# Attention keys and queries stored as half-precision pairs instead of fp32r pairs, with a power of two on the keys and its inverse on the queries

## The chip, the cores and the metric

The kernel runs on one core of one Trainium2 chip. The metric is device time in microseconds of one execution. The kernel before was timed three times: 3205.57 us is the median, 3202.81 and 3209.93 us are the ends. One further execution was taken by the hardware profiler; all rows in this document come from such profiled executions.

TensorE (PE in the rows) multiplies; a weight load (PEld) puts the stationary operand into the array before each product. VectorE is DVE, ScalarE is ACT, GpSimd is POOL, and SP is the queue from which most DMAs are issued; POOL issues the others.

## The reference, cut to what matters

Two layers over 2048 tokens of width 1024: a Mamba-2 mixer, then a multi-head latent attention of 16 heads. The part that the change touches is the score of the second layer:

```
ckv, k_rope = split(rms_norm(h, g_kv_in) @ w_dkv, [256])
kv = (rms_norm(ckv, g_ckv) @ w_ukv).reshape(B, S, 16, 64 + 64)
k_nope, v = split(kv, [64]);  k_rope = apply_rope(k_rope, cos, sin)
q = (rms_norm(cq, g_q) @ w_uq).reshape(B, S, 16, 64 + 32)
q_nope, q_rope = split(q, [64]);  q_rope = apply_rope(q_rope, ...)
s = einsum(q_nope, k_nope) + einsum(q_rope, k_rope)      # 96 channels in all
p = softmax(where(mask, s * 96 ** -0.5, -inf));  o = einsum(p, v)
```

So every head has keys and queries of 96 channels (64 of its own, 32 turned by the rotary table, of which the keys' 32 are shared by the heads), and a causal mask. Inputs and output are float32.

## The kernel before, in words

**Pairs.** A product in high precision is made of three passes on TensorE: each operand is a pair of a rounded value (hi) and what the rounding left (lo), and `mm3` (lines 84 to 88) adds hi·hi, hi·lo and lo·hi into one bank of PSUM. Its lines 86, 87 and 88 are therefore the lines of nearly all large products. Two kinds of pairs are in use. `split` (lines 106 to 113) makes pairs in F32R, four bytes each: ScalarE writes hi, VectorE subtracts (lines 109 and 110, or 112 and 113 with a scale). `pair16` (lines 115 to 118) makes pairs in F16, two bytes each, always with a scale (lines 117 and 118). Mamba's projections, the values V and the probabilities are F16 pairs already; keys and queries are F32R pairs.

**Mamba, about the first 1570 us.** The tokens are cut into 4 blocks of 512 (b), the channels into 4 groups (g); the 16 items (b, g) follow each other in the loop of lines 339 to 369. Beside the state-space scan `ssd` of its item, which has 4 chunks of 5 steps, an iteration emits the output product of the item before (`outp`, 8 steps) and the projections of the item after (`xbc` and `zgate`, together 24 steps). Generators listed in `parts` are run one after the other; after each of their steps, as many steps of `ssd` are emitted as keep `done * total` up with `20 * step`, so the 20 scan steps are spread evenly over `total` steps of the parts. At b = 0, g = 0 and 1, `scan` adds 11 steps that hold no product but one: they load weights, square them on ScalarE with a running sum (line 180) and turn the sum into a power of two (`powers`). In the last block `value_scale` does the like for the values. The order of instructions on each engine comes from a planner, which follows this order of emission as a priority and its own view of durations; the kernel writes no order by hand here. Raw weights pass through the buffer `wraw`, which has 3 slots.

**Latent attention's projections, about 1570 to 2089 us.** For each block of 512 tokens, `mla_kv_down`, `mla_cq`, `mla_up` and `mla_gate` make the latents, the keys, queries and values, and the gate. In `mla_up`, `out` (lines 883 to 886) takes a product of 128 channels by 512 tokens from PSUM, splits it and stores the pair into DRAM through the POOL queue: `kn_d` for the keys, `qn_d` for the queries. `rope` (lines 770 to 781) does so for the turned channels: `kr_d`, `q1_d` and `q2_d`.

**Attention, about 2089 to 3010 us.** For each of 16 heads, `load_k` and `load_q` (lines 939 to 958, POOL queue) bring the head's keys (96 partitions, 2 halves, 2048 tokens) and queries (96, 2, 512 per block) into SBUF, a head ahead of their use. `heads` walks over 4 blocks of 512 queries, each in 4 rows of 128. `cuts` cuts the keys that a row sees into tiles of 512, with a shorter end of 256, 384 or 512; the narrowest width is 256 columns, `max(w, 256)`. That makes 40 tiles in a head: 25 of 512 columns, 7 of 384 and 8 of 256, of which one, the head's first, needs only 128 but is computed with 256. Of every tile:

- `mm3` computes the scores with the queries as weights and the keys as the moving operand (lines 86 to 88, rows `mm<-K,xT`); the last tile of a row gets the mask added by one more product (line 1016, and line 1014 for the head's first tile);
- VectorE takes the maximum (line 1017), then the row's maximum (line 1021);
- ScalarE takes the exponential with its sum (line 1029);
- TensorE transposes it in 128x128 pieces (line 1044), ScalarE and VectorE make an F16 pair of it (lines 117 and 118, rows `PTs<-tr`), and two products with V add into the head's output (lines 1054 and 1055).

TensorE's order in this stage is written by hand: `CREDIT` says after which score tile how many transposes (T) and value products (V) are issued. The orders of VectorE and ScalarE come from the planner. Score tiles and transposes share 8 banks of PSUM, so TensorE can run ahead of ScalarE by few tiles only.

**The output projection** takes the rest, from about 3010 us, and is not touched.

Of the kernel before, what the change touches and what calls it, by code (L numbers as in the profile page):

```python
# [69 lines left out]
class Net:  # L70
# [180 lines left out]
    def constants(self, cp):  # L251
        nc, a = self.nc, self.a
        self.pack = cp.tile([P, PACK], F32, name="pack")
        self.idb = cp.tile([P, P], BF16, name="idb")

        self.mk = cp.tile([P, 2 * P], BF16, name="mk")
        at = 0
        for name, n in PACKED:
            setattr(self, name, self.pack[:, at:at + n])
            at += n  # L260

    def layer_constants(self, cp):
# [12 lines left out]
        nc.vector.memset(self.halfpi, TWO_PI / 4)  # L275
        nc.vector.memset(self.mk[:, P:], NEG)
# [3 lines left out]
        self.xdown = cp.tile([P, 1], F32, name="xdown")  # L280
        self.dtdown = cp.tile([P, 1], F32, name="dtdown")
        ss = self.t(self.sm, "ss", [P, 3, 4], bufs=2)[:, 0, :2]
# [13 lines left out]
        nc.vector.tensor_copy(self.idb, self.ident)  # L296
        nc.vector.tensor_copy(self.mk[:, 0:P], self.mask)

# [14 lines left out]
    def mamba(self, cp):  # L313
# [25 lines left out]
        for n, (b, g) in enumerate(items):  # L339
# [32 lines left out]
    def value_scale(self):  # L372
# [4 lines left out]
        for n in range(2):  # L377
# [24 lines left out]
            yield  # L402

    def load_x(self, b, src, tag="hx"):
# [364 lines left out]

    def rope(self, p1, p2, cos, sin, d1, d2, n, t0):  # L770
# [45 lines left out]
    def mla_kv_down(self, b, tables):  # L816
# [10 lines left out]
        for j in range(2):  # L827
# [3 lines left out]
            pk.append(ps)  # L831
        self.rope(pk[0], pk[1], *tables, self.kr_d[0:16], self.kr_d[16:32], 16, b * TB)

# [36 lines left out]
    def mla_up(self, b, tables):  # L870
# [28 lines left out]
        while ahead:  # L899
            (n, w), ahead = ahead, next(todo, None)  # L900
            qT = self.qT
            for i in range(2 if n == 6 else 4):
                r0 = n % 2 * 512 + i * P
                if n < 2:
                    out(chan(cT, w, i, "tr"), self.kn_d[r0:r0 + P])
                elif n < 4:
# [67 lines left out]
    def heads(self, sp):  # L974
# [4 lines left out]
        def cuts(kv):  # L979

            out, at = [], 0
            while at < kv:
                w = min(TB, kv - at)
                if kv - at == TB + P:
                    w = 384
                out.append((at, max(w, 256)))
                at += w
            return out

        def scores(h, qb, st):  # L990
# [8 lines left out]
            for j in range(4):  # L999
# [5 lines left out]
                for n, (c0, w) in enumerate(parts):  # L1005
# [6 lines left out]
                    if n == nb - 1:  # L1012
                        if qb == j == 0:
                            nc.tensor.matmul(s[:, 0:w], self.idb, self.mk, start=False, stop=True)
                        else:
                            nc.tensor.matmul(s[:, w - P:w], self.idb, self.mk[:, 0:P], start=False, stop=True)
                    v.tensor_reduce(mx[:, n:n + 1], s[:, :w], AX.X, ALU.max)  # L1017
# [208 lines left out]
    def run(self):  # L1226
        tc = self.tc
        with ExitStack() as whole:
# [8 lines left out]
            self.ri_d = dp.tile([NH, T], F32, name="ri_d")  # L1237
            self.qn_d = dp.tile([1024, 2, T], F32, name="qn_d")
            self.q1_d = dp.tile([256, 2, T], F32, name="q1_d")
            self.q2_d = dp.tile([256, 2, T], F32, name="q2_d")  # L1240
            self.kn_d = dp.tile([1024, 2, T], F32, name="kn_d")
            self.kr_d = dp.tile([32, 2, T], F32, name="kr_d")
            self.v_d = dp.tile([T, 2048], F16, name="v_d")
# [59 lines left out]
```

## Time and profile before

| | us |
|---|---|
| median of 3 runs | 3205.57 |
| the profiled execution's own time | 3204.34 |
| span of that execution, first to last instruction | 3202.6 |
| Mamba | 0 to 1570 |
| latent projections | 1570 to 2089 |
| attention | 2089 to 3010 |
| output projection | 3010 to 3202.6 |

The mean granted TensorE clock was 0.995 of full speed. A row of a group names the line, the engine, the operation, the output and the inputs with their shapes, the count, the busy time in us with the mean of one in ns, and the idle time of the engine just before, with what ended it. A row of a window gives its length and each engine's busy time in it with the number of instructions, then the granted clock, the share of the DMA engines and their rate. A matmul's shown duration includes a latency that overlaps the next one's, so two durations are compared by their difference, or starts are compared with starts.

### The profile page before, as it was taken

The numbers are of one execution on the slowest core, as the hardware profiler recorded it, in microseconds if no ns is written. First come the engines' busy times: TensorE is split into PE (matmuls) and PEld (weight loads), VectorE is DVE, ScalarE is ACT, GpSimd is POOL, SyncE is SP. The second block draws the span as 40 slices with busy tenths as digits, with TensorE's granted clock in tenths as the row PEclk, the third lists the DMA queues.
The fourth block names the chain that finished last, engine by engine and source line by source line (L and its number), as shares of the span: only waits on it lengthen the run. The fifth ranks groups of instructions, "written<-read, shape, count | busy, mean of one in ns | idle before, by whom it ended". The sixth has DMA issues, their size and how long they took to land.

```text
span 3202.6 us, 51345 instructions
## 1 busy us (share of the span) xinstructions
PE 3085.4 (96%) x17744; PEld 2163.4 (68%) x17744; DVE 2401.2 (75%) x5178; ACT 1914.1 (60%) x4817; POOL 609.1 (19%) x842
## 2 busy tenths in 40 slices
PE   6999999999999999999999999999999999999998
PEld 3455555666655566665878888877777777777777
DVE  7778887767677676767876665678888888888675
ACT  8667554444455444455645554477877778778522
POOL 0212122121122212212111211322212122222100
PEclk9999999999999999999999999999999999999999
DMA  8667645334443345334476656853444434443485
GB/s 285 229 214 230 229 144 194 127 126 145 141 157 130 115 151 189 127 128 142 141 271 218 225 190 194 265 111 78 95 81 84 81 78 96 79 97 99 101 270 159
DMA packets 207113, 497.61 MB, mean 155 GB/s; under 512 B 27746, under 2 KB 51042, under 8 KB 205412
## 3 DMA queue, kind: packets, MB, share of 16 engines
q1 hardware_dynamic: 165444, 370.04, 35.6%
q0 software_dynamic: 41408, 124.29, 15.9%
q8 instruction: 140, 2.29, 0.3%
q14 instruction: 121, 0.99, 0.1%
HBM read 362.22 MB, written 131.99 MB: 154 GB/s over the span
## 4 chain that ended last, share of the span: by engine, by line
PE 64%; DVE 13%; ACT 8%; DMA 8%; issue 6%; POOL 1%; SPq 0%; ACTq 0%; DVEq 0%; POOLq 0%
PE mm L86 13%; PE mm L87 12%; PE mm L88 12%; PE tr L1044 6%; PE tr L87 3%; PE tr L1054 3%; PE tr L1055 3%; PE tr L86 3%; PE tr L88 3%; DVE cacc L460 3%; DMA big<-cumT 2%; DMA wraw<-in_ssm_w_in_dram 1%; DVE big L634 1%; ACT Pr L1029 1%; PE tr L656 1%
## 5 line engine op out<-in xcount | busy, mean ns | idle before, releaser
L118 DVE SCALAR_TENSOR_TENSOR PTs<-tr,PTs 128x512 f16<-128x512 f32 (+3 forms) x640 | 374.9, 607 | 93.9 <-ACT PTs L117 86.8
L117 ACT ACTIVATE PTs<-tr 128x512 f16<-128x512 f32 (+3 forms) x640 | 328.5, 541 | 141.4 <-PE tr L1044 140.3
L1017 DVE TENSOR_REDUCE mx<-mm 128x1 f32<-128x512 f32 (+2 forms) x631 | 375.7, 608 | 45.7 <-PE mm L88 42.6
L1029 ACT ACTIVATE Pr<-mm,nm 128x512 f32<-128x512 f32 (+2 forms) x631 | 395.7, 636 | 23.1 <-DVE nm L1021 21.4
L1044 PE MATMUL tr<-pack,Pr 128*128 128x128 f32 x2176 | 317.6, 273 | 1.0 <-ACT Os L1061 0.9
L86 PE MATMUL mm<-K,xT 96*128 96x512 f32 (+2 forms) x639 | 288.2, 451 | 23.3 <-ACT Pr L1029 21.8
L86 PE MATMUL mm<-xT,wsp 128*128 128x512 f16 (+1 forms) x800 | 304.9, 381 | 0.3 <-DVE sz L484 0.3
L88 PE MATMUL mm<-xT,wsp 128*128 128x512 f16 (+1 forms) x800 | 303.4, 380 | 1.4 <-DVE wsp L118 1.3
L87 PE MATMUL mm<-xT,wsp 128*128 128x512 f16 (+1 forms) x800 | 303.7, 380 | 0.0
L1044 PEld LDWEIGHTS tr<-pack,Pr 128*128 128x128 f32 x2176 | 253.5, 141 | 49.7 <-ACT Os L1061 1.7
L648 ACT ACTIVATE Xw<-tr,d_wend 128x64 f32<-128x64 f32 x512 | 183.4, 359 | 133.3 <-DVE Xd L644 133.3
L460 DVE SCALAR_TENSOR_TENSOR cacc<-craw,pack,cacc 128x512 f32<-128x512 f32 x288 | 213.6, 764 | 30.5 <-ACT cacc L458 28.9
L86 PE MATMUL mm<-wsp,xT 128*128 128x512 f16 (+1 forms) x640 | 232.4, 363 | 1.6 <-ACT craw L454 1.6
L88 PE MATMUL mm<-K,xT 96*128 96x512 f32 (+2 forms) x639 | 231.6, 362 | 0.0
L87 PE MATMUL mm<-wsp,xT 128*128 128x512 f16 (+1 forms) x640 | 231.6, 362 | 0.0
L87 PE MATMUL mm<-K,xT 96*128 96x512 f32 (+2 forms) x639 | 231.4, 362 | 0.0
L88 PE MATMUL mm<-wsp,xT 128*128 128x512 f16 (+1 forms) x640 | 231.1, 362 | 0.0
L1054 PE MATMUL tr<-PTs,xT 128*128 128x512 f16 (+3 forms) x640 | 222.0, 348 | 0.1
L86 PE MATMUL mm<-wsp,yT 128*128 128x512 f32 x512 | 208.1, 409 | 13.3 <-DVE sz L484 4.7
L1055 PE MATMUL tr<-PTs,xT 128*128 128x512 f16 (+3 forms) x640 | 219.4, 347 | 0.0
L606 POOL TENSOR_TENSOR Xp<-Xw,Xp 128x512 fp32r<-128x512 f32 x64 | 81.8, 1278 | 711.3 <-ACT Xp L605 382.4
L88 PE MATMUL mm<-wsp,yT 128*128 128x512 f32 x512 | 203.0, 397 | 1.4 <-DVE yT L110 1.4
(411 smaller groups left out, 7418.2 us busy)
## 6 DMA issues: line engine op xcount, KB each, us to landing
wsp<-wi_d SPq DMA_DIRECT2D x96, 512.0 KB, 3.7
wsp<-wo_d SPq DMA_DIRECT2D x96, 512.0 KB, 3.5
big<-cumT SPq DMA_DIRECT2D x64, 512.0 KB, 4.9
wi_d<-wsp SPq DMA_DIRECT2D x32, 512.0 KB, 3.4
wo_d<-wsp SPq DMA_DIRECT2D x64, 256.0 KB, 2.5
xT<-qn_d POOLq DMA_DIRECT2D x64, 256.0 KB, 4.4
K<-kn_d POOLq DMA_DIRECT2D x15, 1024.0 KB, 9.2
hx<-in_ssm_w_in_dram SPq DMA_DIRECT2D x48, 256.0 KB, 4.3
```

The source lines that it names most:

```text
L86: mm(out, l_hi, r_hi, start=start, stop=False)
L87: mm(out, l_hi, r_lo, start=False, stop=False)
L88: mm(out, l_lo, r_hi, start=False, stop=stop)
L117: self.nc.scalar.activation(hi, src, AF.Copy, scale=scale)
L118: self.nc.vector.scalar_tensor_tensor(lo, src, scale, hi, ALU.mult, ALU.subtract)
L460: nc.vector.scalar_tensor_tensor(acc, raw[:, k:k + TB], wk[k], acc, ALU.mult, ALU.add)
L648: act(Xw[:, hc], px[:, hc], AF.Copy, scale=wend[:, h0 + h:h0 + h + 1])
L1017: v.tensor_reduce(mx[:, n:n + 1], s[:, :w], AX.X, ALU.max)
L1029: nc.scalar.activation(x[:, :w], s[:, :w], AF.Exp, bias=nm, accum_out=sm[:, n:n + 1])
L1044: nc.tensor.transpose(pt[:, j * P:(j + 1) * P], st["P"][j][kb], self.ident)
L1054: nc.tensor.matmul(st["O"][:, c], vals[h][:, kb, :], u[:, 0], start=kb == 0, stop=False)
L1055: nc.tensor.matmul(st["O"][:, c], vals[h][:, kb, :], u[:, 1], start=False, stop=kb == nk - 1)
```

## The change

Keys and queries become F16 pairs. The DRAM arrays `kn_d`, `kr_d`, `qn_d`, `q1_d`, `q2_d` and the SBUF tiles `K` and `xT` of the queries are F16; `out` and `rope` call `pair16` in place of `split`. So that neither side leaves the range of F16, the keys are multiplied by one power of two, `ku`, in `pair16`'s scale, and the queries by its inverse, which is multiplied into `gqs`, the gain that the query latents have anyway. `ku` is computed by a new generator `head_scale` from the weights' squared sums, as one more part of the item b = 1, g = 0. It has 22 steps and counts 22 in `total`: 21 loads (13 of 128x512, 8 of 128x32) through `wraw` with a square on ScalarE each, and one step of small operations with one tiny product. In `cuts` the least width of 256 is gone, so that the head's first tile has 128 columns, the wide mask tile is gone with its line 1014, and `mk` is half as wide.

```diff
@@ mamba
+            if b == 1 and g == 0:
+                parts.append(self.head_scale())
+                total += 22
@@
+    def head_scale(self):
+        nc, v, a = self.nc, self.nc.vector, self.a
+        ss = self.t(self.sm, "hs", [P, 3, 12], bufs=1)
+        pieces = [(0, a["kv_w_up"][k * P:(k + 1) * P, c * TB:(c + 1) * TB], self.gkl[:, k:k + 1])
+                  for k in range(2) for c in range(2)]
+        pieces += [(2, a["mla_w_uq"][k * P:(k + 1) * P, c * TB:(c + 1) * TB], self.gqs[:, k:k + 1])
+                   for k in range(3) for c in range(3)]
+        pieces += [(1, a["kv_w_down"][k * P:(k + 1) * P, 256:288], self.gk[:, k:k + 1]) for k in range(KD)]
+        at = [0, 0, 0]
+        for i, src, gain in pieces:
+            n = src.shape[1]
+            raw = self.t(self.wp, "wraw", [P, TB], bufs=WRAW)
+            nc.sync.dma_start(raw[:, :n], src)
+            nc.scalar.activation(self.t(self.sp, "yt", [P, D], BF16, bufs=2)[:, :n], raw[:, :n], AF.Square,
+                                 scale=gain, accum_out=ss[:, i, at[i]:at[i] + 1])
+            at[i] += 1
+            yield
+        x = self.t(self.sm, "hx", [P, 2], bufs=1)
+        for i in range(3):
+            v.tensor_reduce(ss[:, i, 0:1], ss[:, i, :at[i]], AX.X, ALU.add)
...
+        nc.tensor.matmul(ps[:, 0:2], self.ones, x, start=True, stop=True)
...
+        v.tensor_scalar(self.ku.bitcast(I32), e[:, 2:3], 23, None, ALU.logical_shift_left)
...
+        v.tensor_scalar(self.gqs, self.gqs, x[:, 0:1], None, ALU.mult)
+        yield
@@ rope (and the call for the keys passes self.ku[:16])
-            u = self.ev()
-            self.split(u[:n, 0, :], u[:n, 1, :], x[:n])
-            nc.gpsimd.dma_start(d[:, :, t0:t0 + TB], u[:n].bitcast(F32))
+            u = self.ev(F16)
+            self.pair16(u[:n, 0, :], u[:n, 1, :], x[:n], scale)
+            nc.gpsimd.dma_start(d[:, :, t0:t0 + TB], u[:n])
@@ mla_up (and the call for the keys passes self.ku)
-        def out(ps, d):
-            u = self.ev()
-            self.split(u[:, 0, :], u[:, 1, :], ps)
-            nc.gpsimd.dma_start(d[:, :, t0:t0 + TB], u.bitcast(F32))
+        def out(ps, d, scale=1.0):
+            u = self.ev(F16)
+            self.pair16(u[:, 0, :], u[:, 1, :], ps, scale)
+            nc.gpsimd.dma_start(d[:, :, t0:t0 + TB], u)
@@ load_k, load_q
-            self.keys[h] = self.t(self.hp, "K", [96, 2, T], F32R, bufs=2)
+            self.keys[h] = self.t(self.hp, "K", [96, 2, T], F16, bufs=2)
-        Q = self.quer[h, n] = self.t(self.xq, "xT", [96, 2, TB], F32R, bufs=8)
+        Q = self.quer[h, n] = self.t(self.xq, "xT", [96, 2, TB], F16, bufs=8)
@@ cuts
-                out.append((at, max(w, 256)))
+                out.append((at, w))
@@ scores
-                        if qb == j == 0:
-                            nc.tensor.matmul(s[:, 0:w], self.idb, self.mk, start=False, stop=True)
-                        else:
-                            nc.tensor.matmul(s[:, w - P:w], self.idb, self.mk[:, 0:P], start=False, stop=True)
+                        nc.tensor.matmul(s[:, w - P:w], self.idb, self.mk, start=False, stop=True)
@@ run: qn_d, q1_d, q2_d, kn_d, kr_d
-            self.kn_d = dp.tile([1024, 2, T], F32, name="kn_d")
+            self.kn_d = dp.tile([1024, 2, T], F16, name="kn_d")
```

More of the change, by code (lines that the diff above doesn't have):

```diff
@@ L254, in constants @@
         self.idb = cp.tile([P, P], BF16, name="idb")
-        self.mk = cp.tile([P, 2 * P], BF16, name="mk")
+        self.mk = cp.tile([P, P], BF16, name="mk")
         at = 0
@@ L275, in layer_constants @@
         nc.vector.memset(self.halfpi, TWO_PI / 4)
-        nc.vector.memset(self.mk[:, P:], NEG)
         self.wdt = cp.tile([P, KD, 2, H], F16, name="wdt")
@@ L280, in layer_constants @@
         self.xdown = cp.tile([P, 1], F32, name="xdown")
+        self.ku = cp.tile([P, 1], F32, name="ku")
         self.dtdown = cp.tile([P, 1], F32, name="dtdown")
@@ L296, in layer_constants @@
         nc.vector.tensor_copy(self.idb, self.ident)
-        nc.vector.tensor_copy(self.mk[:, 0:P], self.mask)
+        nc.vector.tensor_copy(self.mk, self.mask)
     def layers(self):
@@ L768, in rope_tables, with rope @@
         return cos, ang
-    def rope(self, p1, p2, cos, sin, d1, d2, n, t0):
+    def rope(self, p1, p2, cos, sin, d1, d2, n, t0, scale=1.0):
         nc, v = self.nc, self.nc.vector
@@ L831, in mla_kv_down @@
             pk.append(ps)
-        self.rope(pk[0], pk[1], *tables, self.kr_d[0:16], self.kr_d[16:32], 16, b * TB)
+        self.rope(pk[0], pk[1], *tables, self.kr_d[0:16], self.kr_d[16:32], 16, b * TB, self.ku[:16])
     def mla_cq(self, b):
@@ L904, in mla_up @@
                 if n < 2:
-                    out(chan(cT, w, i, "tr"), self.kn_d[r0:r0 + P])
+                    out(chan(cT, w, i, "tr"), self.kn_d[r0:r0 + P], self.ku)
                 elif n < 4:
@@ L1237, in run @@
             self.ri_d = dp.tile([NH, T], F32, name="ri_d")
-            self.qn_d = dp.tile([1024, 2, T], F32, name="qn_d")
-            self.q1_d = dp.tile([256, 2, T], F32, name="q1_d")
-            self.q2_d = dp.tile([256, 2, T], F32, name="q2_d")
-            self.kn_d = dp.tile([1024, 2, T], F32, name="kn_d")
-            self.kr_d = dp.tile([32, 2, T], F32, name="kr_d")
+            self.qn_d = dp.tile([1024, 2, T], F16, name="qn_d")
+            self.q1_d = dp.tile([256, 2, T], F16, name="q1_d")
+            self.q2_d = dp.tile([256, 2, T], F16, name="q2_d")
+            self.kn_d = dp.tile([1024, 2, T], F16, name="kn_d")
+            self.kr_d = dp.tile([32, 2, T], F16, name="kr_d")
             self.v_d = dp.tile([T, 2048], F16, name="v_d")
```

11 lines of the change are left out of this document (added).

## The prediction, made before the changed kernel was run

> **What bounds the kernel now.** I read the page's busy shares first, then the windows by stage and by head, then the groups of attention with shapes kept apart, and last the timeline of a few microseconds.
>
> ```profile
> PE 3085.4 (96%) x17744; PEld 2163.4 (68%) x17744; DVE 2401.2 (75%) x5178; ACT 1914.1 (60%) x4817; POOL 609.1 (19%) x842
> ...
> core 0: us, PE busy (x) PEld busy (x) DVE busy (x) ACT busy (x) POOL busy (x), PEclk, DMA share, GB/s
> 1570.00:2089.00 519.00, 508.74 (x2542) 432.09 (x2541) 337.51 (x668) 266.60 (x503) 97.58 (x158) 1.00 0.68 223
> 2555.00:2612.30 57.30, 56.03 (x356) 42.99 (x354) 48.30 (x115) 45.38 (x128) 12.07 (x19) 1.00 0.42 84
> ```
>
> TensorE is the bound: busy for 96% of the span, the next engine for 75%. In attention one head takes 57.2 us, of which it is busy 56.0; VectorE is next with 48.3. A saving on TensorE there is worth its full size until VectorE's 48.3 us, or the order in which the engines wait for each other, comes in the way.
>
> Is a busy TensorE at its own limit, or held by its weight loads? The timeline of two short stretches answers:
>
> ```profile
> 2500.29 0.38 PE L1055 MATMUL tr<-PTs,xT 128*128 128x512 f16 x1
> ...
> 2500.32 0.59 PE L86 MATMUL mm<-K,xT 96*128 96x512 f32 x1
> ...
> 2500.74 0.40 PE L87 MATMUL mm<-K,xT 96*128 96x512 f32 x1
> ...
> 2510.74 0.28 PE L86 MATMUL mm<-K,xT 96*128 96x256 f32 x1
> 2510.86 0.28 PE L87 MATMUL mm<-K,xT 96*128 96x256 f32 x1
> ```
>
> Passes of 256 columns start 120 ns apart. And L86 shows 0.59 us only because its start is shown early: from the start of L1055 to the start of L87 lie 0.45 us, which hold both passes.
>
> **Term 1, the score passes.** The same product with F16 operands is in the trace, in the value products next door:
>
> ```profile
> L1055 PE MATMUL tr<-PTs,xT 128*128 128x512 f16 x448 | 169.8, 379 | 0.0
> L87 PE MATMUL mm<-K,xT 96*128 96x512 f32 x395 | 155.6, 394 | 0.0
> L1016 PE MATMUL mm<-mk,idb 128*128 128x128 bf16 x238 | 54.9, 231 | 0.0
> L87 PE MATMUL mm<-K,xT 96*128 96x384 f32 x110 | 37.1, 337 | 0.0
> L86 PE MATMUL mm<-K,xT 96*128 96x256 f32 x126 | 38.1, 302 | 0.6 <-ACT Pr L1029 0.5
> L87 PE MATMUL mm<-K,xT 96*128 96x256 f32 x126 | 35.6, 283 | 0.0
> L1055 PE MATMUL tr<-PTs,xT 128*128 128x384 f16 x64 | 20.9, 326 | 0.0
> L1055 PE MATMUL tr<-PTs,xT 128*128 128x256 f16 x64 | 17.4, 273 | 0.0
> L1055 PE MATMUL tr<-PTs,xT 128*128 128x128 f16 x64 | 14.0, 219 | 0.0
> L1014 PE MATMUL mm<-mk,idb 128*128 128x256 bf16 x15 | 4.2, 283 | 0.0
> ```
>
> The durations hold the same overlapped latency, so their differences are the saving of a pass. 512 columns: 394 - 379 = 15 ns; 400 tiles of 3 passes give 18.0 us. 384: 337 - 326 = 11 ns; 112 x 3 gives 3.7 us. 256: 283 - 273 = 10 ns; 112 x 3 gives 3.4 us. The head's first tile goes from 256 to 128 columns: 302 + 2 x 283 + 283 ns (with its mask product) become three times 219 and 231, 263 ns less, 4.2 us over 16 heads. The sum is 29 us. If the 450 ns above less 2 x 215 is right for L86, each triple has some 5 ns more, so I put the upper end at 33 us.
>
> How much of it arrives? TensorE has a gap of 1.3 us in each head (57.3 less 56.03). What ends it stands in the first row below: an exponential on ScalarE frees the bank of the next score tile. That exponential waits for the row's maximum, and that for the row's last product; no F16 pass lies in this chain behind that product, so I leave the gap as it is. In the densest stretch, the second row, VectorE has little to give:
>
> ```profile
> L86 PE MATMUL mm<-K,xT 96*128 96x512 f32 x395 | 202.2, 512 | 22.5 <-ACT Pr L1029 21.3
> ...
> 2536.00:2546.00 10.00, 10.00 (x72) 8.14 (x69) 9.35 (x29) 8.59 (x27) 0.85 (x2) 1.00 0.64 129
> ```
>
> A head would lose 29/16 = 1.8 us, 3%; in this stretch 0.3 us of 10, and VectorE has 0.65. It fits, but barely, since both engines wait for each other in turn. I take 25 of 29 us; the lower end is 12, where more than half of each head gives nothing. VectorE's and ScalarE's orders are replanned and could differ by some tenths of a microsecond per head either way; that is inside these ends.
>
> The weight loads of the score passes get shorter too, though by the starts above they lie under the passes and count nothing in this term:
>
> ```profile
> L87 PEld LDWEIGHTS mm<-K,xT 96*128 96x128 f32 x631 | 120.1, 190 | 8.4
> L1055 PEld LDWEIGHTS <-xT 128*128 128x128 f16 x640 | 62.7, 98 | 14.8 <-issue 0.2
> ```
>
> The Trainium skill, in TensorE: Matmul & The Clock Gate, under Weight-path perf modes, says that a full load of 128 weights that aren't FP32 goes by a fast path, measured as about twice as fast. The trace agrees with the speed, 98 against 190 ns; what it would make of the time, were the loads in the way, is one of the rivals below.
>
> **Term 2, the new part head_scale.** It gives TensorE nothing to do but one tiny product, and it stretches the scan of item (1, 0): with 54 steps in place of 32, only 20 x 32 / 54, 12 of the 20 scan steps, are emitted beside the projections; 8 come beside loads and squares alone. What lies behind is `outp` of the same item, which needs the scan's results. The like exists in items (0, 0) and (0, 1): there 35 steps with 24 of products leave 6 uncovered, and 43 with 32 leave 5.
>
> ```profile
> 157.00:187.00 30.00, 22.96 (x146) 17.29 (x144) 23.34 (x70) 25.87 (x71) 3.85 (x4) 0.87 0.88 275
> 260.00:292.00 32.00, 25.92 (x163) 19.10 (x162) 25.70 (x74) 28.03 (x73) 2.60 (x2) 0.95 0.85 282
> 536.00:566.00 30.00, 29.38 (x168) 15.63 (x166) 24.30 (x53) 17.44 (x41) 8.31 (x11) 1.00 0.30 99
> ...
> 167.00:172.00 5.00, 5.00 (x33) 4.12 (x30) 2.07 (x5) 3.16 (x9) 1.28 (x1) 0.50 0.73 232
> ```
>
> The ends of (0, 0) and (0, 1) idle 7.0 and 6.1 us against 0.6 at the end of (1, 0) today, and in the first the clock fell to 0.50 for 5 us, which cost another 2.5. So 9.5 us over 6 steps and 6.1 over 5, 1.6 and 1.2 us for each. With 8 steps that would be 10 to 13 us. But those ends also had 85% of the DMA engines in use, longer squares and weight splits in ScalarE's queue (28 us busy of 32, against 17 of 30 in the third row), so I take 9 us. The lower end is 2 us: ScalarE has 12 idle us in the third row's stretch and may square early. The upper end is where the loads go round one after another: 21 loads through 3 slots are 7 rounds, each a landing and a square.
>
> ```profile
> hx<-in_ssm_w_in_dram SPq DMA_DIRECT2D x48, 256.0 KB, 4.3
> ...
> L180 ACT ACTIVATE yt<-hx 128x1024 bf16<-128x1024 f32 x30 | 31.8, 1064 | 3.9 <-DMA hx<-in_ssm_w_in_dram 2.1 <-DVE y L663 1.8
> L239 ACT ACTIVATE yt<-xs 128x384 bf16<-128x384 f32 x16 | 8.2, 527 | 0.1
> ```
>
> About 4.3 us and, for 512 columns, some 0.7 us with the sum's reading: 5 us a round, 35 us. Less 3 us of products of `outp` that are ready by then (I put them at 12 passes of 0.23 us), that is 32. On SP's queue the 21 loads stand ahead of later weight loads and of the scan's `big<-cumT`; on ScalarE the scan's operations stand behind a square that waits for its load. That is how the upper end would come about.
>
> The Trainium skill says under The HAM clock gate of the same page that TensorE's clock goes to half after an idle window of about 3.4 us. The window at 167 agrees: granted clock 0.50 after the gaps ahead of it; by that rule alone, one long gap at the end of item (1, 0) would cost a few microseconds beyond itself.
>
> **Term 3, eviction, stores and loads.** `pair16` in place of `split`:
>
> ```profile
> L109 ACT ACTIVATE big<-mm 128x512 fp32r<-128x512 f32 x12 | 7.2, 599 | 9.4 <-PE mm L88 9.2
> L117 ACT ACTIVATE big<-tr 128x512 f16<-128x512 f32 x12 | 7.1, 596 | 5.7 <-PE tr L88 4.8 <-ACT xs L863 0.7
> L112 ACT ACTIVATE yT<-tr,pack 128x512 fp32r<-128x512 f32 x12 | 7.4, 692 | 0.0
> ```
>
> 596 for 599 ns, and VectorE subtracts from PSUM as before: nothing for the queries. With a scale from a tile ScalarE takes about 692, so 32 stores of keys cost 3 us there, beside TensorE, which is the bound of that stage with 508.7 of 519 us while ScalarE has 266.6. Were that cover gone, it would be those 3 us. Stores and loads move half the bytes on the POOL queue; attention's idle TensorE waits for no DMA in any row of term 1, and the stage before idles 10 us in all. I take 0, from 3 us won to 3 lost.
>
> **The sum.** Against the profiled execution's own 3204.34 us: -25 + 9 + 0 = 3188.3. The runs' median lies 1.2 us above that execution, so 3189.5, rounded to 3189.
>
> **The rivals.**
>
> Replanned order (chance 0.16): VectorE's queue is in order, and an exponential or a maximum planned behind a pair that waits for transposes holds the next score tile; then each head's gap grows by what the passes save. For it: the dense stretch, VectorE 9.35 of 10. Against: 48.3 of 57.3 over a head. With 10 of 29 us arriving: 3205.57 - 10 + 9, about 3204, no change.
>
> The loads of head_scale go one after another (0.09): the upper end of term 2, at the end of item (1, 0), about 540 to 600 us. It decides once that idle time passes 25 us. For it: three slots, squares queued between the scan's operations. Against: for the loads of `scan`, ScalarE waited 2.1 us over 30 squares. Then 3205.57 - 25 + 32 + 2.5 for the halved clock, about 3215, slower.
>
> Weight loads in the way (0.07): if the 118 ns by which L86's mean duration exceeds L87's (512 against 394) were load and not an early shown start, part would go with faster loads: 92 ns (190 - 98) on 640 tiles, 59 us more, so about 3131. Against it: the 450 ns for two passes above. This is what the rule of Weight-path perf modes in the Trainium skill's page would come to here.
>
> head_scale is absorbed (0.10): term 2 near 2 us and term 1 near 29; about 3178.
>
> **How the numbers follow.** The forecast itself has 0.58, and its own range from the ends of the terms is 3175 to 3200. About 0.2% (6.4 us) is what a measurement of this kernel can tell from no change. Faster than 3199.2: 0.56 of the forecast's 0.58, the absorbed case, the weight loads, together 0.73. Within: 0.02 of the forecast and 0.14 of the replanned order, 0.16. Slower: the loads and 0.02 of the replanned order, 0.11. The range of 8 in 10 is 3170 to 3207: it takes in the replanned order and leaves out the weight loads and the serial loads.
>
> **What would show it.** Term 1: rows `mm<-K,xT` in F16 with 380 ns for lines 87 and 88, weight loads of 98 ns, a head of about 55.6 us in place of 57.2, and a gap per head still near 1.3 us; a gap of 3 us would be the replanned order. Term 2: the window of 30 us that ends with item (1, 0) idles about 9 us and its clock dips. Term 3: the stage of the projections stays at 519 us. The forecast is wrong if the head shrinks by under 0.8 us, or if item (1, 0) and the next lose over 20 us.

## The result, and the profile after

The changed kernel takes 3185.82 us, the median of four runs (3185.80 to 3190.25); the kernel before took 3204.94 us beside it (3202.81 to 3209.93). The ratio is 0.9942, with a 95% interval of 0.9924 to 0.9959. So the kernel became 19 us faster; the prediction said 3189.

The page of the kernel after has this row of busy shares:

```profile
PE 3059.6 (96%) x17746; PEld 2046.3 (64%) x17746; DVE 2394.7 (75%) x5191; ACT 1929.9 (61%) x4859; POOL 610.5 (19%) x842
```

TensorE is the bound as before, with 26 us less of busy time, and the busy time of its weight loads fell by 117 us. The time is in four places, which the windows cut at the same events show: the start of item (1, 0), where `head_scale` is, to the start of item (1, 1); from there to the start of item (1, 3); from Mamba's last product to the first score; from the first score to the start of the last head's closing transpose (line 1073 before, 1110 after). Columns are as in the prediction's windows (length, busy time of PE, PEld, DVE, ACT and POOL with their instructions, clock, DMA share, GB/s). First the kernel before:

```profile
475.80:566.50 90.70, 89.75 (x535) 54.08 (x534) 64.03 (x127) 44.70 (x120) 19.94 (x24) 1.00 0.55 188
566.50:771.50 205.00, 201.70 (x1173) 124.63 (x1172) 144.97 (x295) 95.55 (x253) 37.85 (x48) 0.99 0.38 129
1553.80:2088.00 534.20, 523.46 (x2647) 444.40 (x2645) 350.24 (x697) 280.37 (x539) 101.28 (x163) 1.00 0.68 222
2088.00:3011.80 923.80, 899.40 (x5654) 686.89 (x5654) 772.71 (x1831) 733.59 (x2009) 201.82 (x296) 1.00 0.42 84
```

Then the kernel after; the fifth row is one head:

```profile
475.20:587.40 112.20, 101.06 (x568) 62.01 (x567) 64.24 (x130) 56.78 (x162) 16.82 (x24) 0.94 0.55 184
587.40:784.40 197.00, 192.84 (x1140) 117.50 (x1140) 145.92 (x308) 95.39 (x253) 38.24 (x48) 1.00 0.39 134
1567.40:2093.10 525.70, 522.88 (x2646) 445.87 (x2645) 352.62 (x697) 283.64 (x539) 106.63 (x170) 1.00 0.57 183
2093.10:2993.80 900.70, 871.55 (x5656) 567.37 (x5654) 763.79 (x1831) 734.27 (x2009) 198.97 (x289) 1.00 0.27 60
...
2556.00:2611.60 55.60, 54.14 (x354) 35.33 (x353) 47.45 (x115) 45.29 (x126) 12.16 (x19) 1.00 0.29 58
```

| stretch | before | after | difference | forecast |
|---|---|---|---|---|
| item (1, 0) and the next two | 295.7 | 309.2 | +13.5 | +9 |
| latent projections | 534.2 | 525.7 | -8.5 | 0 |
| attention | 923.8 | 900.7 | -23.1 | -25 |
| all the rest | | | -0.4 | 0 |
| profiled execution's own time | 3204.34 | 3185.83 | -18.5 | -16 |

Item (1, 0) alone lost 21.5 us, but 33 of TensorE's instructions moved into it from the items behind (535 to 568 in the first row, 1173 to 1140 in the second), so these two rows are read together. Attention gave what was forecast, `head_scale` took half as much again, and the projections gave something that wasn't forecast. The products themselves look as foretold, with shapes kept apart:

```profile
L86 PE MATMUL mm<-K,xT 96*128 96x512 f16 x395 | 150.1, 380 | 24.3 <-ACT Pr L1066 22.4
...
L87 PE MATMUL mm<-K,xT 96*128 96x512 f16 x395 | 149.4, 378 | 0.0
L1053 PE MATMUL mm<-mk,idb 128*128 128x128 bf16 x253 | 55.9, 221 | 0.0
```

And the loads of their weights, in the page's costliest groups:

```profile
L87 PEld LDWEIGHTS <-xT 96*128 96x128 f16 (+1 forms) x1152 | 112.7, 98 | 153.7 <-issue 65.0
```

378 ns for line 87 where 394 stood; 380 for line 86 where 512 stood; 98 ns for a load where 190 stood. The mask's product (line 1053, was 1016) is shorter too, 221 for 231 ns, though nothing in it was changed. The idle time in front of a score tile is still ended by the exponential, 24.3 us where it was 22.5. By these rows alone one would say: the forecast's mechanism, and nothing else. The experiments show that this is not so.

### The profile page after: what moved, and what is told of

Its sections match the earlier page's. It is cut to its first block, busy times and chain, and to the rows that moved or that the text cites. A ratio compares the mean times of both kernels' runs of the same rounds, so it can differ in the third digit from the quotient of the medians.

```text
span 3184.1 us, 51344 instructions
## 1 busy us (share of the span) xinstructions
PE 3059.6 (96%) x17746; PEld 2046.3 (64%) x17746; DVE 2394.7 (75%) x5191; ACT 1929.9 (61%) x4859; POOL 610.5 (19%) x842
## 4 chain that ended last, share of the span: by engine, by line
PE 64%; DVE 13%; ACT 8%; DMA 6%; issue 6%; POOL 1%; SPq 1%; ACTq 0%; DVEq 0%; POOLq 0%
PE mm L86 13%; PE mm L87 12%; PE mm L88 12%; PE tr L1081 6%; PE tr L87 4%; PE tr L86 4%; PE tr L88 3%; PE tr L1092 3%; PE tr L1091 3%; DVE cacc L500 3%; ACT Pr L1066 2%; DMA big<-cumT 2%; DMA wraw<-in_ssm_w_in_dram 1%; DVE PTs L118 1%; DVE big L674 1%
## 5 line engine op out<-in xcount | busy, mean ns | idle before, releaser
L86 PE MATMUL mm<-K,xT 96*128 96x512 f16 (+2 forms) x639 | 222.8, 349 | 27.2 <-ACT Pr L1066 23.7
L88 PE MATMUL mm<-K,xT 96*128 96x512 f16 (+2 forms) x639 | 222.5, 348 | 0.0
L87 PE MATMUL mm<-K,xT 96*128 96x512 f16 (+2 forms) x639 | 221.7, 347 | 0.0
L86 PE MATMUL mm<-wsp,yT 128*128 128x512 f32 x512 | 208.4, 410 | 11.9 <-DVE sz L524 6.3
L87 PEld LDWEIGHTS <-xT 96*128 96x128 f16 (+1 forms) x1152 | 112.7, 98 | 153.7 <-issue 65.0
```

Of the source, the lines that this page charges most:

```text
L86: mm(out, l_hi, r_hi, start=start, stop=False)
L87: mm(out, l_hi, r_lo, start=False, stop=False)
L88: mm(out, l_lo, r_hi, start=False, stop=stop)
```

## The experiments

The kernel before was run again beside each set of experiments; its medians there lie between 3204.94 and 3207.84 us. A difference of 2 or 3 us between kernels of two sets is therefore not to be read.

### The price of head_scale

Two theories for item (1, 0): the scan steps that are emitted beside no product (the forecast's term 2), or the loads going round one after another (a rival). Four kernels tell them apart.

**e1_no_head: no balance at all.**

```diff
-            if b == 1 and g == 0:
-                parts.append(self.head_scale())
-                total += 22
...
+        nc.vector.memset(self.ku, 1.0)
```

> The changed kernel without the part head_scale: the factor is 1 on both sides, so the balance of keys against queries is left out; everything else stays. Theory (head_scale costs what item (1, 0) grew by, 13 us at the end of Mamba): 3185.8 - 13 = 3173 us, the window from 476 us on looks as in the kernel before, and the stage of the projections is as short as in the changed kernel. Rival (the later start only hid waits that come back in the projections, about 8 us there): 3181 us.

Measured: 3170.63 us (3167.47 to 3173.69), ratio to before 0.9887 (0.9873 to 0.9902). `head_scale` therefore costs 15.2 us in the kernel after, or 17.6 by the two ratios (0.9942 less 0.9887).

**e2_before_head: head_scale in the kernel before, its result unused.**

```diff
+            if b == 1 and g == 0:
+                parts.append(self.head_scale())
+                total += 22
...
+        v.tensor_scalar(self.t(self.sm, "hg", [P, 3], bufs=1), self.gqs, x[:, 0:1], None, ALU.mult)
```

> The kernel before with head_scale added at the same place and its result unused, so keys and queries stay F32R pairs. Theory (13 us for head_scale, and the shorter projections come from smaller stores, which this kernel does not have): 3205 + 13 = 3218 us, projections as long as before (518 us from the end of Mamba to the first score). Rival (the shorter projections come from the shifted plan): about 3210 us.

Measured: 3219.97 us (3218.49 to 3222.39), ratio 1.0043 (1.0027 to 1.006), slower than before, 12.1 us above the 3207.84 us beside it. The two prices agree within what can be read, so the cost doesn't hang on what the keys are stored in. I go on with about 15 us.

**e3_pace32: the same part, but the scan paced over 32 steps as before.**

```diff
             if b == 1 and g == 0:
                 parts.append(self.head_scale())
-                total += 22
```

> The changed kernel, but head_scale is not counted in total, so the 20 scan steps of item (1, 0) are all emitted beside the 32 steps of products, and the 21 loads and squares come behind them. Theory (the cost is the 8 scan steps without products beside them): 11 of the 13 us go, about 3175 us. Rival (the cost is the loads going round through 3 slots, with the squares in ScalarE's queue): no change, 3186 us.

Measured: 3174.66 us (3173.48 to 3177.91), ratio 0.9902 (0.9887 to 0.9917): 4.0 us above e1_no_head beside it, so 11 of the 15 us come back by the dropped line alone. All 21 loads and squares are still there, but now behind the scan steps and not among them; so this kernel alone doesn't tell scan steps without products from scan steps held up by squares.

**e4_spread: the 22 steps run beside the projections instead of behind them.**

```diff
-                parts.append(self.head_scale())
-                total += 22
+                parts[1:] = [together(chain(*parts[1:]), self.head_scale())]
```

> The changed kernel with the 22 steps of head_scale emitted one by one beside the 24 steps of projections of item (1, 0), not behind them, and total at 32. Theory of uncovered scan steps: about 3173 us, as without head_scale. Rival of loads through 3 slots and queued squares: the squares now wait for loads among the evacuations of the projections, and the item still loses 5 us or more, 3178 to 3186 us.

Measured: 3169.40 us (3167.12 to 3169.94), ratio 0.9882 (0.9868 to 0.9897): as fast as e1_no_head, which has no such part. Here squares and scan steps share ScalarE's queue again, with products beside them, and loads, squares and the small product cost nothing that can be measured.

The windows of the last 30 us or so of the item, first after, then e4_spread, e1_no_head and e3_pace32:

```profile
557.00:587.00 30.00, 18.86 (x101) 13.65 (x102) 18.68 (x49) 22.30 (x72) 4.99 (x5) 0.78 0.49 146
```

```profile
535.20:565.20 30.00, 29.75 (x172) 16.11 (x170) 25.71 (x64) 18.19 (x43) 6.68 (x10) 1.00 0.40 129
```

```profile
533.30:563.30 30.00, 29.12 (x167) 15.68 (x166) 24.30 (x53) 17.02 (x40) 8.13 (x10) 1.00 0.30 105
```

```profile
550.00:580.00 30.00, 27.66 (x124) 18.37 (x122) 13.10 (x40) 17.34 (x50) 2.74 (x3) 1.00 0.63 203
```

TensorE idles 11.1 us of 30 after, and 0.3, 0.9 and 2.3 in the others. What it waited for is in the waits of that stretch after (us in all, times, longest), and what ScalarE's squares waited for in the view of line 421 (us, times):

```profile
PE tr L723 <- DVE y L718: 5.4, 1, 5.4
PE tr L86 <- ACT Xp L645: 3.1, 1, 3.1
```

```profile
  DMA wraw<-in_mla_w_uq_dram: 2.1, 3
```

Two waits for results of the scan (lines 645 and 718) are 8.5 us of the 11.1. The squares waited 2.1 us for loads, three times. The serial loads would have been rounds of 5 us each; they are refuted. What the longer wait goes back to is in VectorE's waits of the item after:

```profile
DVE big L674 <- DMA big<-cumT: 8.3, 3, 7.0
```

VectorE waited 7.0 us for the scan's own transfer, and then worked without a gap from 573.65 until `y` (line 718) was done at 581.14. That transfer stands behind loads of `head_scale` on SP's queue, which the prediction named as the way to its upper end; but it was issued at 568.40, 0.2 us after the products (line 696) that read its buffer were done, and landed 5.1 us later, against a median of 4.9 for all 64. So the scan's own chain is slow here, and not the loads ahead of it. The wait of 3.1 us is ScalarE's: between 564.7 and 572.6 five squares (3.6 us) and a wait of 1.0 us for a load stand among the copies ahead of `Xp`. So the squares have a part in the price where no product covers them; how large a part was not separated.

The uncovered scan is shown: put the scan steps back beside the products (e3), or the loads and squares as well (e4), and the time goes.

### What the F16 passes are worth, and the order of the maximum

The gap of a head stayed near 1.3 us, but was it the same gap? A short stretch of the timeline after shows one of the longer waits. Columns: start, length, engine, line and operation, and in brackets the wait:

```profile
2541.86 0.68 DVE L1054 TENSOR_REDUCE mx<-mm 128x1 f32<-128x512 f32 x1
...
2542.45 1.28 DVE L118 SCALAR_TENSOR_TENSOR PTs<-tr,PTs 128x512 f16<-128x512 f32 x2
...
2543.65 0.14 DVE L1058 TENSOR_REDUCE nm<-mx 128x1 f32<-128x2 f32 x1
...
2543.83 0.69 ACT L1066 ACTIVATE Pr<-mm,nm 128x512 f32<-128x512 f32 x1 [1.17 <-DVE nm L1058]
```

The tiles' maxima are there at 2542.54. The row's maximum (line 1058), 0.14 us long, could follow at once, but VectorE's plan has two halves of probability pairs (line 118) in front of it; the exponential waits 1.17 us for it. This is the prediction's rival of the replanned order. How much it takes is in the view of the row's maximum, "who waited for it (us, times)"; first before, then after:

```profile
  ACT Pr L1029: 24.2, 34
```

```profile
  ACT Pr L1066: 46.9, 61
```

The waits doubled. Two edits of the plan follow: the first head tile back to 256 columns, and a priority for the row's maximum.

**e7_wide_first: the narrow first tile undone,** with the wide mask and its product as before.

```diff
-                out.append((at, w))
+                out.append((at, max(w, 256)))
```

> The changed kernel with each head's first tile computed with 256 columns again, with the wide mask. By term 1 that tile is worth 4.2 us over 16 heads; in F16 and by starts it is 3 x 53 ns and some 60 ns of the mask, 3.5 us. Theory (TensorE is the bound in that place): about 3189 us. Rival (the place waits for VectorE and ScalarE anyway): 3186 us.

Measured: 3175.01 us (3173.53 to 3176.69), ratio 0.9905 (0.9888 to 0.9921). Computing 128 columns more per head makes the kernel 10.8 us faster, 7.6 of them in the fifteen heads between the first and the last closing transpose (827.1 to 819.5). ScalarE's waits for the row's maximum are back at 24.2 us. The narrow tile saves work, but with it VectorE's order came out differently for the whole head: two or more operations of line 118 stand between the maximum of a row's last tile and the row's maximum in 48 of 256 rows before, in 62 after, and in 48 again in e7_wide_first.

**e8_spread_wide: e4 and e7 together.** 

> The changed kernel with both undoings: head_scale spread beside the projections, and each head's first tile 256 columns wide. If the two effects lie in different stages and add (16 us in Mamba, 9 to 11 us in attention): about 3159 us, heads of 55.06 us. If the attention gain of the wide tile was an accident of that one plan: heads of 55.6 us and 3170 us.

Measured: 3163.71 us (3162.61 to 3165.05), ratio 0.9868 (0.9854 to 0.9883): 5.7 us under e4 and 11.3 under e7. The 16.4 us of e4 and the 10.8 of e7 don't quite add up: 27.2 against 22.1 us from after. The heads are not where the 5 us are missing: from the first to the last closing transpose there are 819.5 us in e7_wide_first and 819.9 in e8_spread_wide. What lies ahead of the first of them differs: e7 comes to it 5.4 us earlier than after does (2161.3 for 2166.7), e8 only 1.1 us earlier than e4 (2150.0 for 2151.1). Why was not settled.

**e9_max_first: the narrow tile kept, the row's maximum planned earlier.**

```diff
-                v.tensor_reduce(nm, mx[:, :nb], AX.X, ALU.max, negate=True)
+                with self.tc.high_priority(20): v.tensor_reduce(nm, mx[:, :nb], AX.X, ALU.max, negate=True)
```

> The changed kernel with one edit: the row's maximum on VectorE (line 1058) gets a priority of 20 in the plan; in the planned order it then stands ahead of one or two probability pairs where it stood behind them, and nothing else moves outside attention. Theory (the narrow first tile costs because the plan put row maxima behind pairs, so that ScalarE's exponentials wait 46.9 us for them against 24.2 us in the kernel before): heads shrink from 55.6 to 55.0 us or less, 3176 us or less. Rival (the narrow tile itself, or the shorter passes, make the wait): heads stay at 55.6 us, 3186 us.

Measured: 3170.10 us (3168.08 to 3172.26), ratio 0.9888 (0.9871 to 0.9904), 15.7 us under after, with the same instructions on every engine. No row's maximum stands behind more than one operation of line 118 here.

**e11_before_max: the same priority in the kernel before.** 

> The kernel before with the row's maximum given the same priority. If the order of the maxima also held the heads there (the 1.3 us gap in each head ends by an exponential that waits for a row maximum): heads under 57.17 us, by up to 1 us, 3190 to 3200 us. If TensorE's passes alone set that head: 57.2 us and 3205 us.

Measured: 3200.38 us (3195.45 to 3204.33), ratio 0.9984 (0.9975 to 0.9994): 5.4 us against the 3205.74 us beside it. The kernel before had a third as much to win from it (a quarter by the windows below).

**e12_wide_max: e7 with the priority.** 

> The changed kernel with the row's maximum given priority and each head's first tile 256 columns wide. With the order of the maxima settled on both sides, its heads against the 57.0 us of the kernel before with the same priority give the F16 passes alone, and the 54.72 us of the narrow tile with that priority against its heads give the narrow tile alone. By starts the passes are worth 2.0 us a head and the narrow tile 0.2 us: heads of 54.95 us, 3172 us in all, 3 us above the same kernel with the narrow tile. If the narrow tile still costs in itself: heads under 54.72 us.

Measured: 3171.31 us (3165.45 to 3172.36), ratio 0.9892 (0.9875 to 0.9909). With the maximum settled, the narrow tile of e9 is worth 1.2 us beside it, which the ranges don't tell from nothing.

The view of the row's maximum in e9_max_first answers to the two above; in e11_before_max it has 11.3 us, 34 times, and in e12_wide_max 11.5 us, 33 times:

```profile
  ACT Pr L1066: 12.7, 35
```

How long the heads are is read between the closing transposes of the first and the last head, fifteen heads. The windows of before, e11_before_max, after, e9_max_first and e12_wide_max:

```profile
2162.60:3011.80 849.20, 827.92 (x5219) 632.55 (x5218) 710.27 (x1672) 675.74 (x1845) 183.99 (x266) 1.00 0.41 83
```

```profile
2157.80:3004.00 846.20, 828.56 (x5220) 632.66 (x5219) 711.09 (x1672) 675.59 (x1845) 183.56 (x266) 1.00 0.41 84
```

```profile
2166.70:2993.80 827.10, 802.06 (x5218) 523.72 (x5218) 702.48 (x1672) 676.22 (x1845) 185.11 (x266) 1.00 0.28 61
```

```profile
2163.90:2978.80 814.90, 797.04 (x5220) 524.57 (x5219) 704.92 (x1672) 672.12 (x1845) 184.57 (x266) 1.00 0.28 61
```

```profile
2158.80:2974.70 815.90, 797.00 (x5221) 526.41 (x5219) 705.21 (x1672) 675.09 (x1845) 184.51 (x266) 1.00 0.28 61
```

Kernels with the same attention agree in this length to 0.9 us: 849.2 in before and e5_half_stores, 827.1 to 828.0 in after, e1_no_head, e4_spread and e6_twice_stored. With the maximum settled on both sides and the same tiles (846.2 to 815.9) the F16 passes are worth 30.3 us over fifteen heads, 32 over sixteen. As it came, 849.2 to 827.1, the whole change was 22.1. The difference went into VectorE's order: after to e9_max_first is 12.2 us, and before to e11_before_max only 3.0. Note the column of TensorE's busy time: 802.06 after, 797.04 in e9, for the same instructions. A matmul that is shown to start early counts a part of its wait as busy, so "busy" is not work, and the gap of 1.3 us a head is not all of the waiting.

**e10_spread_max: e4 and e9 together.** 

> The changed kernel with head_scale spread and the row's maximum given priority, the first tile 128 columns wide. If both causes are right and independent: 3169 less 10 us or more, 3159 us or less.

Measured: 3154.10 us (3152.47 to 3157.36), ratio 0.9839 (0.9825 to 0.9854). It beats both kernels: 31.7 us under after, where e4 (16.4) and e9 (15.7) sum to 32.1; the price of `head_scale` and the order of the maximum are two separate things. Its fifteen heads take 815.2 us, as long as those of e9_max_first (814.9).

### The projections

Term 3 said nothing would come of half as many bytes, since the stage idled only 10 us. It idled 10.7 us before and 2.8 after (the third rows of the result's windows). The waits of TensorE in that stage, first before, then after:

```profile
PE tr L247 <- ACT xs L799: 6.0, 5, 2.1
PE mm L86 <- DMA wsp<-wo_d: 3.9, 3, 2.0
```

```profile
PE tr L247 <- ACT xs L839: 1.2, 1, 1.2
...
PE mm L86 <- DMA wsp<-wo_d: 0.2, 1, 0.2
```

No row here names a store or the POOL queue. In the first, ScalarE copies the latents out of PSUM (`xs`), and this copy was late. In ScalarE's timeline before, what stands ahead of one of these copies is a weight split that waited for a load:

```profile
1730.85 1.31 ACT L109 ACTIVATE wsp<-wraw 128x512 fp32r<-128x512 f32 x2 [2.37 <-DMA wraw<-in_kv_w_up_dram]
1732.07 0.47 ACT L799 ACTIVATE xs<-tr 128x384 f32<-128x384 f32 x1
```

The DMA engines' share in the stage fell from 0.68 to 0.57, and the load of a query weight lands sooner, before and after:

```profile
wraw<-in_mla_w_uq_dram SPq DMA_DIRECT2D x36, 256.0 KB, 4.9
```

```profile
wraw<-in_mla_w_uq_dram SPq DMA_DIRECT2D x36, 256.0 KB, 3.9
```

So in this instance a late load held ScalarE's queue, and with smaller stores the DMA engines had less to do and the loads were faster. Two kernels change the bytes alone.

**e5_half_stores: the kernel before, storing only the hi halves.** The loads put hi into both halves, so that the scores leave out what the rounding left; `rope` and the other four arrays are changed in the same way as the lines shown.

```diff
-            nc.gpsimd.dma_start(d[:, :, t0:t0 + TB], u.bitcast(F32))
+            nc.gpsimd.dma_start(d[:, 0, t0:t0 + TB], u[:, 0].bitcast(F32))
...
-        nc.gpsimd.dma_start(Q[0:64], self.qn_d[h * 64:(h + 1) * 64, :, ts])
+        nc.gpsimd.dma_start(Q[0:64], self.qn_d[h * 64:(h + 1) * 64, 0:1, ts].to_broadcast([64, 2, TB]))
...
```

> The kernel before with only the hi half of each F32R pair of keys and queries stored (half the bytes, as in the changed kernel); the loads bring the hi half into both places of the tile, as many bytes as before, so the lo part is left out of the scores. No head_scale, same passes. Theory (the projections got 8 us shorter because the smaller stores let the weight loads land earlier): about 3197 us, with the waits for wo_d and for the copies of line 799 gone or smaller. Rival (the plan's shift made them shorter): 3205 us.

Measured: 3196.77 us (3196.41 to 3199.66) against 3205.42, ratio 0.9972 (0.9962 to 0.9983): 8.7 us. The waits of the stage:

```profile
PE mm L86 <- DMA wsp<-wo_d: 2.5, 2, 1.9
PE tr L247 <- ACT xs L799: 1.8, 2, 1.5
```

**e6_twice_stored: the kernel after, each store of keys and queries issued a second time** into arrays that nobody reads.

```diff
-            nc.gpsimd.dma_start(d[:, :, t0:t0 + TB], u)
+            nc.gpsimd.dma_start(d[0][:, :, t0:t0 + TB], u)
+            nc.gpsimd.dma_start(d[1][:, :, t0:t0 + TB], u)
```

> The changed kernel with every store of keys and queries issued a second time into a second array, so that as many bytes are stored as before, with twice as many DMA issues on the POOL queue. Theory of the stores: the 8 us come back, about 3193 us. Rival: 3186 us.

Measured: 3190.59 us (3186.25 to 3192.62), ratio 0.995 (0.9935 to 0.9965): 4.8 us above after, with ranges that overlap. The waits of the stage:

```profile
PE tr L247 <- ACT xs L840: 3.0, 3, 1.7
...
PE mm L86 <- DMA wsp<-wo_d: 1.2, 2, 0.7
```

Cut at the same events, the stage is 534.2 us long before, 529.0 in e5_half_stores, 529.4 in e6_twice_stored and 525.7 after. Half the bytes stored take 5.2 us off the kernel before, the doubled ones put 3.7 onto the kernel after, and the same waits move each time. But in e2_before_head, which stores what the kernel before stores, the stage is 531.5. So the bytes are worth some 4 to 5 of the 8.5 us, and 3 us are within what the stage does when only the work ahead of it shifts. What else made up the rest is open. The way by ScalarE's queue is borne out in one direction only: over the whole stage ScalarE waited 59.8 us for raw weights before and 49.9 in e5_half_stores, but 50.1 after and 49.6 in e6_twice_stored. By which way the doubled stores act is open too.

## Why the prediction was right, and where only the sum was

**What bounds the kernel** held: TensorE, in every stage.

**Term 1, the score passes, was undersized, and a loss that it left out cancelled this.** It put 25.1 us on the passes (18.0, 3.7 and 3.4). The runs showed 30.3 us over fifteen heads, 32 over sixteen. The term was worked out from differences of durations, 15, 11 and 10 ns. Starts say more: the passes of 512 columns, before and then after,

```profile
2501.99 0.40 PE L87 MATMUL mm<-K,xT 96*128 96x512 f32 x1
2502.22 0.40 PE L88 MATMUL mm<-K,xT 96*128 96x512 f32 x1
2502.46 0.34 PE L86 MATMUL mm<-K,xT 96*128 96x384 f32 x1
```

```profile
2511.95 0.38 PE L87 MATMUL mm<-K,xT 96*128 96x512 f16 x1
2512.16 0.38 PE L88 MATMUL mm<-K,xT 96*128 96x512 f16 x1
2512.38 0.27 PE L86 MATMUL mm<-K,xT 96*128 96x256 f16 x1
```

follow each other after 0.23 to 0.24 us, and after 0.21 to 0.22. Over the whole stage the medians from a start of line 87 or 88 to the next start are 232 and 215 ns, a saving of 17; for 384 columns 176 and 162, for 256 columns 120 and 109; and the mask's product behind them takes 60 ns for 67. With 400 x 3, 112 x 3 and 128 x 3 passes and 256 masks that is 20.4 + 4.7 + 4.2 + 1.8 = 31.1 us for sixteen heads, against 32 measured. With the 1 us of the narrow tile, the prediction's upper end of 33 was the right value, not an end.

**The narrow first tile** was put at 4.2 us. With the maximum settled it is worth 1.0 us over fifteen heads (815.9 to 814.9), hardly more than such lengths differ by anyway; as it came, with the plan that it brought, it cost 10.8 us. Why it is worth so little even then wasn't tested.

**"I leave the gap as it is"** is the step that failed. The gap that the windows show did stay: 1.3 us in the head before, 1.5 in the head after. But the reason given, that no F16 pass lies in the chain from the row's last product to the exponential, looked only at TensorE's part of the chain. VectorE's part was replanned: the waits for the row's maximum went from 24.2 to 46.9 us. The prediction had this as the rival of the replanned order, priced it at 19 of 29 us lost, and gave it 0.16; it happened at about half that size, 12.2 us less the 3.0 that the kernel before had too. So 9 us of the 32 went there, and 23 arrived where 25 were taken. The forecast's "some tenths of a microsecond per head either way" allowed for it: 0.6 us a head.

**Term 2, head_scale, was right in its mechanism and short in its size:** some 15 us by the runs (15.2 by e1, 12.1 by e2) and 13.5 by the windows, for the 9 that were taken, inside the ends of 2 and 32. Its own rows gave 10 to 13 us for 8 uncovered steps; it took less because ScalarE has more room there than at the ends of items (0, 0) and (0, 1). That discount was wrong. By the windows a step cost 13.5 / 8 = 1.7 us, more than the 1.2 and 1.6 that it was scaled from, and the longest wait (5.4 us) was for VectorE, which ScalarE's room doesn't shorten; the next (3.1 us) was for ScalarE itself. By the windows, idle time in the item and the next two grew from 4.2 to 15.3 us, by 11.1, and TensorE was busy 2.4 us longer with the same 1708 instructions (291.5 to 293.9), most likely by the halved clock; the prediction had foretold that 2.5 beside its rival, not in its own sum. One of its readings is wrong: the window at 167, where it saw the rule of an idle window borne out, has no gap ahead of it longer than 1.3 us.

**Term 3, stores and loads, taken as 0 with 3 either way,** was worth 8.5 us. "Attention's idle TensorE waits for no DMA" is true and beside the point; of the stage before it, it said "idles 10 us in all" and stopped. Of the 10.7 us in the stage's window 7.9 went. What it didn't follow was the releaser's own queue: in the instance shown, the copy that TensorE waited for stood behind a split that waited for a load.

**The rivals.** Serial loads: refuted, since the squares waited 2.1 us for them and the idle time grew by 11.1 us and not by 25. Weight loads in the way: refuted, since they were halved (98 for 190 ns), and of the 59 us more nothing came: the 32 us are explained by the passes' own starts. The 118 ns of line 86 left its duration (380 beside 378 now) without showing in the time, as an early shown start would. Absorbed `head_scale`: refuted as it stands, though e4 shows how it comes true.

**The sum** was 3.2 us off the median and 2.5 off the profiled execution: attention 1.9 us less saved than taken, `head_scale` 4.5 dearer, the projections 8.5 better, the rest 0.4. Inside attention 7 us more from the passes, 3 less from the narrow tile and 9 lost to VectorE's order stand against the 4 of 29 us that the forecast held back. The sum was right; its first term was right only because its errors cancelled, and the errors of the other two cancelled in part. So the sign and the main cause were foreseen, and that the sum came this close is luck. The forecast's own range of 3175 to 3200 doesn't follow from the ends of its terms, either: 12 us won and 9 lost give 3203, with 32 lost 3226.

## What to carry to other kernels

When operands get faster, follow the chain through every engine's order, not only the one that got faster: a short operation on which the bound waits (here a 0.14 us maximum) is worth a priority of its own, and a change of one tile's size can move it behind long work in all heads. A serial part that is paced over work that holds no products leaves the bound uncovered, here at 1.7 us a step; put such work beside products, where it cost nothing here. Compare starts with starts, since durations and busy time both hold waiting.

## What the runs showed of the hardware that was not expected

**Passes with operands in four bytes took longer than F16 passes, and so did the product behind them.** From start to start 232 against 215 ns for 512 columns, 176 against 162 for 384, 120 against 109 for 256, though the load of weights (190 ns, 98 in F16) is shown beside other passes; and a bf16 product of the mask behind three such passes takes 67 ns to the next start, behind F16 passes 60. Whether the columns stream more slowly or something of the load stays in the way isn't told apart here.

**The clock stayed at half while the gaps went on.** The clock fell at about 573.8 us, after a gap of 3.1 us. Short windows after show what followed:

```profile
575.00:578.00 3.00, 0.92 (x2) 0.20 (x1) 3.00 (x8) 2.16 (x8) 1.33 (x2) 0.50 0.11 16
578.00:581.00 3.00, 0.00 (x0) 0.00 (x0) 3.00 (x8) 0.74 (x3) 0.00 (x0) 0.50 0.04 5
581.00:584.00 3.00, 1.75 (x6) 1.22 (x6) 1.51 (x3) 3.00 (x10) 0.00 (x0) 0.50 0.11 16
584.00:587.00 3.00, 3.00 (x10) 2.35 (x9) 1.56 (x12) 0.61 (x4) 0.00 (x0) 0.50 0.75 203
587.00:590.00 3.00, 2.18 (x14) 1.67 (x12) 2.57 (x15) 0.74 (x4) 0.00 (x0) 0.93 0.88 316
```

It came back in the last of these rows, behind the one that is full of work: 13.6 us at half speed in all, for which TensorE paid some 2.4 us, since it was idle through more than half of it. The Trainium skill, in TensorE: Matmul & The Clock Gate, under The HAM clock gate, says that it takes a window of about 3.4 us of sustained work to come back, as it takes an idle one to fall; both agree with these rows to within a microsecond.

**Stores on one queue delay loads on another.** With half the bytes stored from POOL's queue, SP's 256 KB loads of a query weight went from 4.9 us before to 4.1 in e5_half_stores; with the stores doubled (e6_twice_stored) they went from 3.9 us after to 5.1.
